# Another order for the projections, output rows and head buffers of a model's two mixing layers

## The chip, the cores and the metric

The kernel runs on one core of one Trainium2 chip. The metric is the device time of one execution in microseconds (us); lower is better.

## The reference

Two models of depth two run behind each other on 256 tokens of width 1024, in float32. The change concerns the second model's two mixing layers. Cut to what matters, one of them is:

```python
h = rms_norm(x, norm_mix_pre)
za, zq, zkv, zg, zc, zd = split(h @ w_in)
y_conv = silu(layer_norm(dwconv31(a * sigmoid(gate))))        # a, gate = halves of za
y_nsa = g0 * o_cmp + g1 * o_slc + g2 * o_win                  # 4 heads of 64, keys and values from zkv, g from zg
y_sgu = u * (w_s @ layer_norm(v) + b)                         # u, v = halves of gelu(zc)
y_pool = ((windowed means of zd) - zd) @ w_p * scale
x = x + rms_norm(concat(y_conv, y_nsa, y_sgu, y_pool) @ w_out)
```

`o_cmp` attends to 15 compressed blocks of keys; `o_slc` and `o_win` are causal attention over all 256 tokens here, with two different sets of keys and values. A feed-forward layer with its own norms follows each mixing layer.

## The kernel before

**Products.** A float32 weight is split into a high and a low part (`whi`, by ScalarE; `wlo`, by VectorE), activations likewise (`hh`/`hl`, `oh`/`ol`), and each product is three TensorE matmuls (`mm3`, line 821). Weights stream from memory through four buffers `wraw`; a chunk has one or two units of 128 x 1024, and at most six or seven converted units wait for use. `_plan` (line 138) lists the chunks in the order of use; `_weights` (line 68) takes those of the mixing layers from `MIX_ORDER` and `MIX_ROWS` (lines 57 and 58). One unit feeds 24 matmuls of 256 columns, a projection of 256 columns 48.

**Order of work.** Instructions are put on each engine's queue by a planner that runs on the host: a main line emits projections and output rows one after the other, and between their parts (`step`, line 787) it advances generators, which hold the elementwise chains, and converts further weights (`tick`, line 780). A generator goes on when its inputs are due by the planner's clock (`on`, line 766). The convolution's taps on VectorE come last: they fill what is left (`conv_gen`, line 1810).

**A mixing layer** (`mix`, line 2113). `begin` (line 999) computes the convolution's inputs ag0 and ag1 while the norm's statistics come in, and then makes the normalised input slice by slice, 8 slices of 128 channels, in `hh`/`hl` (`make_h`, line 939). Later projections read these. Then the main line follows `MIX_ORDER`:

- v and u: the gating's two halves. Their GELU is on ScalarE; `sgu_gen` (line 1901) does norm, spatial product and split, into slices 4 and 5 of `oh`/`ol`.
- conv: 18 of the 31 taps of one half of the convolution, as products with diagonal matrices. They wait for the gated input (`gated_input`, line 2147). The other taps are VectorE's; the norm, SiLU and split follow, into slices 0 and 1.
- cvf, kk, cw1, q, cvt: the heads' projections: inputs of the compression, keys (rotated, `rope2_gen`), the compression itself with raw weights (`nsa_cmp`, line 1951), queries, values and gates.
- zd: the pooled part's input; `pool_gen` (line 1870) does two small products, a scaling and the split, into slices 6 and 7.

**Heads** (`nsa_heads`, line 1980) run in two pairs, as generators that start once keys, queries, values and compression are there. A pair makes logits (TensorE), masks and maxima (VectorE), exponentials with sums (ScalarE), scaling by the gates (VectorE), transposes into `PT` (TensorE, copied by ScalarE), the products with the values, and the split into slices 2 and 3. Both pairs share the buffers `P` (probabilities) and `PT`; one mark, `busy`, is held from a pair's logits to its products with the values, so pair 2 begins behind pair 1's products.

**Rows.** The output projection takes four PSUM banks (`mm4`) and runs in four groups of 48 matmuls, one for each part: 0 is the convolution, 1 the heads, 2 the gating, 3 the pooled part. `MIX_ROWS` orders them; a group is emitted once its part is stored. The last group is followed at once by the norm behind the layer (`post`, line 1733).

Rows of the trace all carry one line number, 427, that of the call that records each operation; so work is followed by its tiles. `banks` is PSUM, `sv` and `su` the gating's v and u, `cs` the convolution's result before the split, `kp` the keys, `kr` and `qr` rotated keys and queries, `ps` the scaled pooled result (`banks<-pb,ar` is its last product), `cst,ar` a transpose of probabilities, `ar<-sg,gy` the gated input.

Of the kernel before, what the change touches and what calls it, by code (L numbers as in the profile page):

```python
# [53 lines left out]

FOX_ORDER = '0 1 f v0 2 3 v1 4 5 v2 6 7 v3'.split()

MIX_ORDER = 'v u conv cvf kk cw1 q cvt zd'.split()
MIX_ROWS = (2, 3, 0, 1)


DIL_TOKENS = ((3, 3, 3), (3, 3, 3), (3, 3, 3), (1, 1, 3))
# [6 lines left out]
def _weights(seg):  # L68
# [34 lines left out]
    elif kind == "mix":  # L103
        for which in ["ag0", "ag1"] + [w for w in MIX_ORDER if w != "conv"]:
            n = 1 if which in ("cvf", "kk") else 2
            out.append((("cw1", l) if which == "cw1" else ("mixt" if which in ("v", "cvt", "zd") else "mix", l, which), n))
        for c in MIX_ROWS:
            out.append((("row", ("w_out_2", (l,)), c * 256), 2))
# [561 lines left out]
class K:  # L670
# [1309 lines left out]
    def nsa_heads(self, t, q, qr, kr, vt, kc, vc, gates, pvs):  # L1980

        nc = self.nc
        half = [slice(0, 64), slice(64, 128)]

        where = {(0, 1): (0, 128), (1, 1): (128, 256), (0, 2): (384, 128), (1, 2): (512, 256),
                 (0, 0): (768, 16), (1, 0): (784, 16)}
        P, PT = self.PP, self.PT
        nm, sm, cf = self.small(12, "nm"), self.small(12, "sums"), self.small(12, "cf")
        cm = self.c("causal")

        while self.busy:
            yield
        self.busy.add(0)
        yield from self.on("pe", qr, kr, kc)
        for parts in (((0, 1), (1, 1)), ((0, 2), (1, 2), (0, 0), (1, 0))):
            L = yield from self.bank(2)
            o0 = where[parts[0]][0]
            for qt, br in parts:
                c0, n = where[qt, br]
                qs = slice(qt * 128, qt * 128 + 128)  # L2000
                for e, r in enumerate(half):
                    o = L[:, e, c0 - o0:c0 - o0 + n]
                    if br:
                        nc.tensor.matmul(o, qr[r, t, qs], kr[r, br - 1, :n], start=True, stop=True)
                    else:
                        nc.tensor.matmul(o[:, :15], q[r, t, qs], kc[r], start=True, stop=True)
            for e in range(2):
                n = 384 if len(parts) == 2 else 415
                yield from self.on("dve", L[:, e, :n], out=[P[e][:, o0:o0 + n]])
                for qt, br in parts:  # L2010
                    c0, n = where[qt, br]
                    i = e * 6 + qt * 3 + br
                    n = n if br else 15
                    if br:
                        mask = cm[:, 0:128] if qt == 0 else cm[:, 128:384]
                    else:
                        mask = self.c("cmask")[:, qt * 16:qt * 16 + 15]
                    nc.vector.tensor_tensor_reduce(P[e][:, c0:c0 + n], L[:, e, c0 - o0:c0 - o0 + n], mask, -1.0, CAP, OP.add,
                                                   OP.min, nm[:, i:i + 1])
            self.rel(L)  # L2020
        for e in range(2):
            yield from self.on("act", P[e])
            for (qt, br), (c0, n) in where.items():
                i = e * 6 + qt * 3 + br
                n = n if br else 15
                nc.scalar.activation(P[e][:, c0:c0 + n], P[e][:, c0:c0 + n], AF.Exp, scale=-1.0, bias=nm[:, i:i + 1],
                                     accum_out=sm[:, i:i + 1])
        yield from self.on("dve", sm)
        nc.vector.reciprocal(cf, sm)
        for e in range(2):  # L2030
            c3 = cf[:, 6 * e:6 * e + 6].rearrange("p (t b) -> p t b", t=2)
            h = 2 * t + e
            nc.vector.tensor_tensor(c3, c3, gates[:, :, h * 3:h * 3 + 3], op=OP.mult)
        for e in range(2):
            c = cf[:, 6 * e:6 * e + 6]
            for o, n, i in ((768, 15, 0), (0, 128, 1), (128, 256, 4)):
                if i == 0:
                    for qt in range(2):
                        p = P[e][:, 768 + 16 * qt:783 + 16 * qt]
                        nc.vector.tensor_scalar(p, p, c[:, 3 * qt:3 * qt + 1], None, op0=OP.mult)  # L2040
                    continue
                p = P[e][:, :768].rearrange("p (b n) -> p b n", b=2)[:, :, o:o + n]
                nc.vector.tensor_tensor(p, p, c[:, i:i + 2][:, :, None].to_broadcast([128, 2, n]), op=OP.mult)
        for e in range(2):
            pT = PT[:, e * 1024:e * 1024 + 1024]
            yield from self.on("pe", P[e])
            T = yield from self.bank()
            for i in range(4):
                nc.tensor.transpose(T[:, i * 128:i * 128 + 128], P[e][:, i * 128:i * 128 + 128], self.c("ident"))
            yield from self.on("act", T, out=[pT[:, 0:512]])  # L2050
            nc.scalar.copy(pT[:, 0:512], T)
            self.rel(T)
            T2 = yield from self.bank()
            for i in range(2):
                nc.tensor.transpose(T2[:, i * 128:i * 128 + 128], P[e][:, 512 + i * 128:640 + i * 128], self.c("ident"))
            for i in range(2):
                nc.tensor.transpose(T2[:15, 256 + i * 128:384 + i * 128], P[e][:, 768 + 16 * i:783 + 16 * i],
                                    self.c("ident"))
            yield from self.on("act", T2)
            nc.scalar.copy(pT[:, 512:768], T2[:, 0:256])  # L2060
            nc.scalar.copy(pT[:15, 768:1024], T2[:15, 256:512])
            self.rel(T2)
        yield from self.on("pe", PT)
        pv = yield from self.bank()
        x = PT.rearrange("p (e n) -> p e n", e=2)
        self.pv2(pv, [([vt[:, kt, br * 64:br * 64 + 64]] * 2, x[:, :, br * 384:br * 384 + 384], kt)
                      for br in range(2) for kt in range(2)], False)
        for e in range(2):
            nc.tensor.matmul(pv[64 * e:64 * e + 64, :S], vc, PT[:15, e * 1024 + 768:e * 1024 + 1024], start=False, stop=True,
                             skip_group_check=True)  # L2070
        self.busy.remove(0)
        pvs[t] = pv
        yield from self.o_store(pvs, 2 * t, 2 + t)
        if t:
            self.stored.add(1)
# [37 lines left out]
    def mix(self, l, norm, following):  # L2113
# [131 lines left out]
        def heads():  # L2245
            for t in range(2):
                self.pending.append((lambda: len(ready) == 3 and len(cmp) == 2,
                                     self.nsa_heads(t, v3(q), qr, kr, vt, kc, vc, gates, pvs)))
# [9 lines left out]
        heads()  # L2258
        for w in MIX_ORDER:
            f[w]()  # L2260
# [3 lines left out]
        def rows(i, c, after=None):  # L2264
            for half in range(2):
                self.wait(lambda: c in self.stored)
                w = self.st.get("row", ("w_out_2", (l,)), c * 256)
                x = (self.oh[:, 2 * c:2 * c + 2], self.ol[:, 2 * c:2 * c + 2])
                self.rows(acc, half, w, *x, i == 0, i == 3, after)
                if i < 3:  # L2270
                    self.tick()

        for i in range(3):
            rows(i, MIX_ROWS[i])
        return self.post(acc, lambda after: rows(3, MIX_ROWS[3], after), self.v("n_mix_post", l * 8, 8), following)

# [102 lines left out]
```

## Time and profile before

| | |
|---|---|
| median of 3 runs | 1850.83 us (1848.05 to 1851.8) |
| the profiled execution | 1849.76 us, span 1848.0 us |
| mean granted TensorE clock of the profiled execution | 0.996 |
| busy: TensorE matmul / weight load / VectorE / ScalarE | 98% / 95% / 80% / 54% |
| the chain that ended last | TensorE 67%, issue 18%, VectorE 10%, ScalarE 5% |
| first mixing layer: its first projection behind `begin` to its last rows | about 1231 to 1327 us |
| second mixing layer: the same | about 1544 to 1640 us |

PE is TensorE's matmul, PEld its weight load, DVE VectorE, ACT ScalarE, SP the queue that issues the weight loads. In a timeline a row shows start and length in us, engine, operation, output and inputs, shapes and count; the brackets at its end hold the idle time of that engine before it and what ended it. Ends of matmuls are modelled; their starts are measured.

### The profile page before, as it was taken

What the parts mean: (1) busy time and instruction counts of PE and PEld (TensorE: products, weight loads), DVE (VectorE), ACT (ScalarE), POOL (GpSimd) and SP (SyncE); (2) the same over time, 40 slices, a digit from 0 to 9 for tenths busy, and PEclk for the clock granted to TensorE, in tenths of its full rate; (3) what the DMA queues carried; (4) which work ended last, traced back from release to release, by engine and by line L of the source; (5) the groups of instructions that cost most, each with busy time, mean ns of one, the idle gap of its engine ahead of it and who ended that gap; (6) DMA issues with size and microseconds to landing.
All of it is one profiled execution on the core that took longest, in us unless ns stands there. A gap on an engine that the chain in (4) does not pass through costs nothing.

```text
span 1848.0 us, 36709 instructions
## 1 busy us (share of the span) xinstructions
PE 1801.9 (98%) x15239; PEld 1755.8 (95%) x15239; DVE 1479.2 (80%) x2696; ACT 1006.4 (54%) x1706; POOL 42.7 (2%) x51
## 2 busy tenths in 40 slices
PE   8999999999999999999999999999999999999997
PEld 7999999999999999999999999998899998889997
DVE  7978798898779867779788965589698779879876
ACT  4544568644454445555555654454676554566653
POOL 0200010000000000000000000000000000000000
PEclk9999999999999999999999999999999999999999
DMA  9889375499848973433333566533255543325550
GB/s 392 307 347 341 116 291 184 162 364 352 312 151 343 340 277 129 183 137 122 143 125 138 208 244 223 185 135 137 92 195 210 183 160 137 115 87 204 212 183 24
DMA packets 54474, 378.36 MB, mean 205 GB/s; under 512 B 6305, under 2 KB 7809, under 8 KB 9506
## 3 DMA queue, kind: packets, MB, share of 16 engines
q1 hardware_dynamic: 52992, 372.42, 54.5%
q0 software_dynamic: 1168, 3.46, 0.6%
q8 instruction: 119, 1.95, 0.4%
q14 instruction: 49, 0.40, 0.1%
q10 hardware_dynamic: 146, 0.14, 0.0%
HBM read 374.89 MB, written 1.05 MB: 203 GB/s over the span
## 4 chain that ended last, share of the span: by engine, by line
PE 67%; issue 18%; DVE 10%; ACT 5%; POOL 1%; DMA 0%; POOLq 0%; DVEq 0%; ACTq 0%
PE banks L427 67%; DVE ar L427 3%; DVE wlo L427 2%; ACT ar L427 1%; DVE x L427 1%; ACT whi L427 1%; POOL rz L427 1%; DVE sq L427 1%; DVE hl L427 1%; ACT L427 1%; ACT hh L427 1%; ACT sq L427 0%; DVE ht L427 0%; DVE rs L427 0%; DVE ol L427 0%
## 5 line engine op out<-in xcount | busy, mean ns | idle before, releaser
L427 DVE TENSOR_TENSOR wlo<-wraw,whi 128x1024 fp32r<-128x1024 f32 x557 | 669.8, 1220 | 173.8 <-ACT whi L427 172.8
L427 PE MATMUL banks<-hh,whi 128*128 128x256 f32 (+1 forms) x2792 | 792.2, 284 | 2.3 <-ACT whi L427 1.1
L427 PE MATMUL banks<-hh,wlo 128*128 128x256 f32 (+1 forms) x2792 | 782.4, 281 | 2.9 <-DVE wlo L427 2.9
L427 PE MATMUL banks<-hl,whi 128*128 128x256 f32 (+1 forms) x2792 | 782.2, 281 | 0.8 <-DVE hl L427 0.8
L427 ACT CAST whi<-wraw 128x1024 fp32r<-128x1024 f32 x557 | 569.4, 1048 | 181.6 <-DMA wraw<-w 93.4
L427 PEld LDWEIGHTS banks<-hh,whi 128*128 128x128 f32 x2792 | 525.6, 188 | 6.0 <-ACT hh L427 2.3
L427 PEld LDWEIGHTS banks<-hh,wlo 128*128 128x128 f32 x2792 | 526.0, 189 | 3.7 <-DVE wlo L427 3.7
L427 PEld LDWEIGHTS banks<-hl,whi 128*128 128x128 f32 x2792 | 526.4, 189 | 1.4 <-DVE hl L427 1.4
L427 PE MATMUL banks<-oh,whi 128*128 128x256 f32 x1312 | 372.7, 284 | 7.8 <-DVE x L427 3.5
L427 PE MATMUL banks<-ol,whi 128*128 128x256 f32 x1312 | 368.3, 281 | 4.0 <-DVE ol L427 3.8
L427 PE MATMUL banks<-oh,wlo 128*128 128x256 f32 x1312 | 367.7, 280 | 0.0
L427 PEld LDWEIGHTS banks<-oh,whi 128*128 128x128 f32 x1312 | 247.1, 188 | 15.6 <-DVE x L427 6.0
L427 PEld LDWEIGHTS banks<-ol,whi 128*128 128x128 f32 x1312 | 247.3, 188 | 4.9 <-DVE ol L427 4.9
L427 PEld LDWEIGHTS banks<-oh,wlo 128*128 128x128 f32 x1312 | 247.3, 188 | 0.0
L427 DVE CUSTOM_DVE_ANT_0 wraw<-wraw,cb 128x1024 f32<-128x1024 f32 x128 | 152.0, 1216 | 0.0
L427 ACT ACTIVATE sg<-banks 128x256 f32<-128x256 f32 x82 | 31.4, 384 | 163.9 <-PE banks L427 163.8
L427 PE MATMUL banks<-whi,hh 128*128 128x256 f32 x352 | 102.2, 290 | 1.6 <-ACT hh L427 1.4
L427 PE MATMUL banks<-whi,hl 128*128 128x256 f32 x352 | 99.1, 282 | 0.1
L427 PE MATMUL banks<-wlo,hh 128*128 128x256 f32 x352 | 98.8, 281 | 0.0
L427 DVE SCALAR_TENSOR_TENSOR cy<-cs,vec,cy 128x255 f32<-128x255 f32 (+1 forms) x176 | 83.7, 481 | 7.8 <-ACT cy L427 4.7
L427 DVE TENSOR_TENSOR sg<-banks,sg 128x256 f32<-128x256 f32 x82 | 34.4, 422 | 62.7 <-ACT sg L427 62.6
L427 ACT ACTIVATE cy<-cs,vec 128x256 f32<-128x256 f32 x88 | 47.9, 594 | 49.6 <-DVE cs L427 48.8
(214 smaller groups left out, 1734.1 us busy)
## 6 DMA issues: line engine op xcount, KB each, us to landing
wraw<-w SPq DMA_DIRECT2D x342, 1024.0 KB, 4.9
ar<-w SPq DMA_DIRECT2D x8, 1024.0 KB, 9.1
wraw<-w SPq DMA_DIRECT2D x5, 512.0 KB, 3.3
ar<-lw POOLq DMA_DIRECT2D x2, 752.0 KB, 5.1
x<-x SPq DMA_DIRECT2D x2, 512.0 KB, 4.8
out<-x SPq DMA_DIRECT2D x8, 128.0 KB, 1.9
ar<-bands POOLq DMA_DIRECT2D x1, 544.0 KB, 8.1
ar<-dm POOLq DMA_DIRECT2D x1, 512.0 KB, 9.1
```

The lines of the kernel that those rows point to most:

```text
L427: return f(out, *args, **kw)
```

## The change

Three things change. The projections are emitted as cvf, kk, conv, cw1, q, cvt, zd, v, u: the heads' first, then the pooled part, then the gating. The output rows come as pooled, gating, convolution, heads. And the heads hold two marks: 0 for the probabilities, from a pair's logits until its transposes are copied, and 1 for the transposed ones, from before the transposes to the products with the values. The weights' order in memory and on the load queue follows the first two.

```diff
-MIX_ORDER = 'v u conv cvf kk cw1 q cvt zd'.split()
-MIX_ROWS = (2, 3, 0, 1)
+MIX_ORDER = 'cvf kk conv cw1 q cvt zd v u'.split()
+MIX_ROWS = (3, 2, 0, 1)
@@ nsa_heads
-        while self.busy:
+        while 0 in self.busy:
             yield
         self.busy.add(0)
         yield from self.on("pe", qr, kr, kc)
...
                 nc.vector.tensor_tensor(p, p, c[:, i:i + 2][:, :, None].to_broadcast([128, 2, n]), op=OP.mult)
+        while 1 in self.busy:
+            yield
+        self.busy.add(1)
         for e in range(2):
             pT = PT[:, e * 1024:e * 1024 + 1024]
             yield from self.on("pe", P[e])
...
             self.rel(T2)
+        self.busy.remove(0)
         yield from self.on("pe", PT)
         pv = yield from self.bank()
...
-        self.busy.remove(0)
+        self.busy.remove(1)
         pvs[t] = pv
```

## Rows read from the trace of the kernel before

**Rows 1.** The page, busy us, share of the span and instructions by engine.

```profile
PE 1801.9 (98%) x15239; PEld 1755.8 (95%) x15239; DVE 1479.2 (80%) x2696; ACT 1006.4 (54%) x1706; POOL 42.7 (2%) x51
```

**Rows 2.** Busy by stretches: us; PE, PEld, DVE, ACT, POOL; clock; DMA share, GB/s.

```profile
1231.00:1283.10 52.10, 51.63 (x438) 48.40 (x437) 49.94 (x120) 26.75 (x55) 0.00 (x0) 1.00 0.49 182
...
1295.19:1303.36 8.17, 8.17 (x49) 6.83 (x49) 1.23 (x1) 5.29 (x10) 0.00 (x0) 0.63 0.36 129
...
1610.32:1615.67 5.35, 5.35 (x49) 4.31 (x49) 1.23 (x1) 3.99 (x8) 0.00 (x0) 1.00 0.57 199
```

**Rows 3.** Timeline of TensorE, first layer, around the pooled part's rows.

```profile
1291.10 1.03 PE L427 MATMUL banks<-pb,ar 128*128 128x256 f32 x4
1293.71 0.38 PE L427 MATMUL banks<-oh,whi 128*128 128x256 f32 x1 [1.58 <-ACT oh L427]
1295.19 0.58 PE L427 MATMUL banks<-ol,whi 128*128 128x256 f32 x1 [1.10 <-DVE ol L427]
```

**Rows 4.** Timeline of TensorE, second layer, pooled rows and pair 2's logits.

```profile
1610.32 0.39 PE L427 MATMUL banks<-ol,whi 128*128 128x256 f32 x1 [1.10 <-DVE ol L427]
...
1618.32 0.93 PE L427 MATMUL banks<-kr,qr 64*128 64x128 f32 x8 [0.89 <-DVE ol L427]
```

**Rows 5.** Timeline of TensorE, first layer, rotation of the keys and pair 2's transposes.

```profile
1257.67 0.70 PE L427 MATMUL banks<-kp,cst 128*128 128x256 f32 x2 [0.47 <-ACT kp L427]
...
1316.06 2.17 PE L427 MATMUL banks<-cst,ar 128*128 128x128 f32 x15 [0.26 <-DVE ar L427]
```

**Rows 6.** Timelines of TensorE and VectorE, start of the first and the second layer.

```profile
1230.93 0.28 PE L427 MATMUL banks<-whi,hh 128*128 128x256 f32 x1
...
1236.74 0.75 DVE L427 SCALAR_TENSOR_TENSOR ar<-sg,gy 128x256 f32<-128x256 f32 x2
...
1544.15 0.39 PE L427 MATMUL banks<-whi,hh 128*128 128x256 f32 x1 [1.41 <-ACT hh L427]
...
1549.10 0.42 DVE L427 TENSOR_TENSOR hl<-ht,hh 128x256 fp32r<-128x256 f32 x1 [0.19 <-ACT hh L427]
...
1550.86 0.28 PE L427 MATMUL banks<-whi,hl 128*128 128x256 f32 x1
1550.98 0.28 PE L427 MATMUL banks<-hh,whi 128*128 128x256 f32 x1
...
1552.91 0.75 DVE L427 SCALAR_TENSOR_TENSOR ar<-sg,gy 128x256 f32<-128x256 f32 x2
```

**Rows 7.** Timelines of ScalarE, TensorE and VectorE, first layer, the gating's chain.

```profile
1242.57 0.60 ACT L427 ACTIVATE su<-banks 128x512 f32<-128x512 f32 x1 [1.06 <-PE banks L427]
...
1243.70 1.14 PE L427 MATMUL banks<-ar,sv 128*64 128x128 f32 x16
...
1246.47 1.22 DVE L427 TENSOR_TENSOR wlo<-wraw,whi 128x1024 fp32r<-128x1024 f32 x1
1247.61 0.68 DVE L427 TENSOR_TENSOR ol<-sy,oh 128x512 fp32r<-128x512 f32 x1
```

**Rows 8.** Timeline of ScalarE, first layer: pair 1's exponentials, and the SiLU.

```profile
1277.76 1.28 ACT L427 ACT_TABLE_LOAD   x1 [1.74 <-DVE nm L427]
...
1283.65 0.19 ACT L427 ACTIVATION_READ_ACCUMULATOR ar<-ar,nm 128x1 f32 x1
...
1300.81 1.28 ACT L427 ACT_TABLE_LOAD   x1
1302.11 1.02 ACT L427 ACTIVATE cs<-banks,vec 128x256 f32<-128x256 f32 x2
```

**Rows 9.** First layer, convolution's end and its rows (timelines); heads' work (groups by tile).

```profile
1303.81 0.69 DVE L427 TENSOR_TENSOR ol<-cs,oh 128x512 fp32r<-128x512 f32 x1 [1.76 <-ACT oh L427]
...
1309.89 0.28 PE L427 MATMUL banks<-oh,whi 128*128 128x256 f32 x1
...
L427 DVE CUSTOM_DVE_ANT_0 ar<-banks,cst 128x128 f32<-128x128 f32 (+2 forms) x24 | 5.4, 290 | 0.0
L427 DVE TENSOR_TENSOR ar<-ar,cf 128x256 f32<-128x256 f32 (+1 forms) x8 | 4.1, 550 | 0.0
```

## The prediction

> **What bounds the kernel now.** I read the page first: TensorE is busy for 98% of the span [rows 1], so only the small rest, or a slower clock, can be won. The change touches the two mixing layers alone, so the busy table by stretches comes next. In the first layer's projections (1231.00 to 1283.10) TensorE is busy for 51.63 of 52.10 us and VectorE for 49.94 [rows 2]: two engines are full at once. The holes come after it, and the timeline of TensorE names them. The pooled rows wait 1.58 us for the high half of the pooled result and 1.10 us for its low half [rows 3]; the second layer repeats the pair, 1.58 (not shown) and 1.10 [rows 4]. The reader should see why: the pooled projection is the last one before the output rows, and only one group of rows (the gating's) stands between. Right behind these holes the clock falls in the first layer: the same 49 matmuls take 8.17 us at a mean granted clock of 0.63 (part of it at the lower level, 1.2 GHz), and 5.35 us at 1.00 (2.4 GHz) in the second [rows 2]. Smaller holes: 0.47 us ahead of the rotation of the keys, once in each layer; 0.26 us ahead of pair 2's transposes, once in each layer [rows 5]; 0.89 us for a PSUM bank, in the second layer alone [rows 4].
>
> **What the edit removes.** Matmul ends are modelled: in a stream a matmul is listed with 0.28 us while the next starts 0.12 us later [rows 6], so each listed hole is about 0.16 longer.
> - Pooled part. The new order has its projection before v and u, and its rows first. Two projections of 48 matmuls at 0.12, 11.4 us, then cover its chain; 3 us more than now would do. Gone: 1.58 + 1.10 + 2 x 0.16 = 3.0 us per layer, 6.0 in all. Should the cover fail, at most these 3.0 come back.
> - Clock. The holes ahead of the fall are gone, so I take back 8.17 - 5.35 = 2.8 us, once. Its bounds are 0 (another hole pulls it down) and 2.8.
> - Keys. Behind kk stood the compression's weights, with nothing between; now 18 convolution products do. Gone: 0.47 + 0.16 = 0.63 per layer, 1.3.
> - Pair 2. Heads start after cvt, and zd, v, u, 17 us of projections, lie behind them in place of zd alone. By the time the last rows want pair 2 it is long stored. Gone: 0.26 + 0.16 per layer, 0.8. The two marks let pair 2's logits start once pair 1's transposes are copied; in a queue with 17 us of cover this removes no TensorE wait by itself, 0 us (the copies would otherwise be covered too).
> - The bank: 0.89 + 0.16 = 1.05, bounds 0 and 1.05, since PSUM use around it changes; I take it, as two pairs no longer run beside the last rows.
>
> Sum removed: 6.0 + 2.8 + 1.3 + 0.8 + 1.05 = 12.0 us.
>
> **What the edit adds.** No arithmetic; each step is moved with all it issues. On SP's queue the weights go in the new order, cvf and kk as half chunks, and the compression's chunk holds one of four buffers for longer, until its products; behind kk follow the convolution's and the compression's products, which take no converted weights, so the stream gains a lead: 0. On POOL one memset of the blocks moves to an earlier place and has nothing queued behind it there: 0. On TensorE three things are late next.
> - The convolution's products need the gated input. In the first layer the projections start at 1230.93; cvf and kk take 48 x 0.12 = 5.7 and end at 1236.6; the input is written from 1236.74 for 0.75, to 1237.5 [rows 6]. Wait 0.9 us, which v and u (11.4 us) hid before.
> - In the second layer the normalised input is still being made when the projections start at 1544.15 [rows 6]. v takes each of its 8 slices for 6 matmuls (0.72 us), about the pace of making them, and u begins at 1550.98. cvf takes 3 per slice (0.36), so it outruns the maker and ends with it: the last low half is written from 1549.10 for 0.42 [rows 6], cvf ends near 1549.7, kk at 1552.5. The same 48 matmuls ended at 1551.1: 1.4 us lost. Then the gated input: 1552.91 + 0.75 = 1553.7, 1.1 us more. Together 2.5.
> - The gating's rows. u is now the last projection. From the GELU of u (1242.57) to the end of the gating's low half (1247.61 + 0.68) runs 5.7 us [rows 7]. The cover is one group of rows, 48 x 0.12 = 5.7, and the gating's own products, 1.14 [rows 7]: 6.9. But exponentials now run between v's and u's GELUs, so one more activation-table load may stand in the chain, 1.28 [rows 8], and a conversion of 1.2 [rows 7] may be ahead of it on VectorE, half of it on average. Wait: 5.7 + 1.3 + 0.6 - 6.9 = 0.7, rounded up to 1.0 for a queue that is full; 2.0 in all. Bounds: 0 (the load falls elsewhere) and 7.1 per layer (the rival below).
>
> A rule weighed: the load of 1.28 us at 1300.81 is followed by the next activation at 1302.11, 1.30 us in all [rows 8], and that is what I used. The Trainium skill, page "ScalarE: Activation LUTs", section "What ACT_TABLE_LOAD costs", puts a switch at about 2.66 us, load and drain, which speaks against an order with more switches; by it, an estimate, the wait would be 1.4 us longer per layer and the total 2.7 us higher. The row shows no such drain, so the row decides.
>
> Sum added: 0.9 + 2.5 + 2.0 = 5.4 us. Net: 12.0 - 5.4 = 6.6 us less. The profiled execution took 1849.76 us (span 1848.0), so 1843.2; the median of the three runs, 1850.83, is 1.1 above it, so 1844.3.
>
> **Rivals.**
> - Convolution late. Its taps take what VectorE has left, and VectorE is full. Now its low half is ready at 1303.81 + 0.69 = 1304.5 and its rows begin at 1309.89 [rows 9]: 5.4 us to spare. In the new order pair 2's work comes ahead of it, half of 5.4 for masks and half of 4.1 for scaling [rows 9], 4.8 us; and TensorE arrives 3.3 us earlier (half of 6.6). Were all of it in front, 4.8 + 3.3 - 5.4 = 2.7 us of new wait per layer: 1844.3 + 5.4 = 1849.7, no change. For it: 2.2 us idle in 52.1. Against it: the convolution's own chain after the taps sat behind the pooled holes too, and the gating's vector work moves behind it.
> - Slower: the gating behind pair 2. If u's GELU is queued on ScalarE behind pair 2's exponentials, their load and 12 exponentials run from 1277.76 to 1283.65 + 0.19, 6.1 us [rows 8]. It decides once pair 2's masks are done just before u ends. The wait before the gating's rows is then 7.1 us in place of 1.0, in both layers: 1844.3 + 12.2 = 1856.5; and 1862 if the clock falls behind both. At 3.2 us extra per layer the gain is gone. For it: pair 2 may start right around u. Against it: pair 1 starts 17 us of projections before u ends and pair 2 only behind pair 1's transposes, so its exponentials may as well be queued after u's GELU.
> - The order does less than it says: the clock falls anyway, say at the starved start of the second layer, and the bank wait stays: 2.8 + 1.05 back, 1848.2, still barely a gain.
>
> **The numbers.** A measurement of this kernel tells apart about 0.2%, 3.7 us, so faster means under 1847.1. Chances: my forecast 0.64 (1839 with nothing added, 1850.8 - 12.0, up to 1848 with the added waits two thirds larger); convolution late 0.18; the order does less 0.08; gating behind pair 2 0.10. Faster: nearly all of the first (0.62), a third of the second (0.06), half of the third (0.04): 0.72. Slower: 0.08 of the last and 0.02 of the second: 0.10. Same: 0.18. The range takes in the first three: 1839 to 1852; the likeliest case's own is 1839 to 1848.
>
> **What would show it.** In the profile after: no wait of TensorE on the pooled result in either layer; a clock of 1.00 through both layers; about 1 us of wait before the convolution's products; the second layer's first projection stretched to the pace of the normalised input; and, between the pooled and the gating's rows, a wait near 1 us. If that one is over 3 us, or the convolution's rows wait, the sum is wrong there; if the pooled wait stays, the first step is.

## The result and the profile after

The changed kernel takes 1865.8 us (median of 4 runs, 1864.99 to 1866.99) where the kernel before, run beside it, takes 1850.53: a ratio of 1.0083, 95% interval 1.0071 to 1.0096. It is slower by 0.8%; 1844.3 was forecast, with 1852 as the upper end. The profiled execution took 1866.99 us (span 1865.2).

The page's busy row, the answer to [rows 1]: the same matmuls, two more instructions on ScalarE, and TensorE's share one point lower.

```profile
PE 1809.7 (97%) x15239; PEld 1765.1 (95%) x15239; DVE 1479.8 (79%) x2696; ACT 1009.9 (54%) x1708; POOL 42.7 (2%) x51
```

Busy by stretches comes next, with one stretch for each mixing layer: from the norm's spread products (`banks<-cst,rz`) to the end of the last output rows. Columns as in [rows 2]. First the kernel before, then the changed one.

```profile
1224.69:1327.04 102.35, 98.72 (x807) 90.73 (x808) 82.16 (x215) 56.80 (x126) 0.79 (x1) 0.97 0.39 145
1542.02:1640.42 98.40, 91.75 (x759) 82.99 (x760) 80.78 (x214) 54.16 (x124) 0.79 (x1) 1.00 0.41 150
sum 200.75, PE 190.48 PEld 173.72 DVE 162.94 ACT 110.95 POOL 1.58; mean PE 95.24 PEld 86.86 DVE 81.47 ACT 55.48 POOL 0.79
```

```profile
1226.35:1333.63 107.28, 97.67 (x807) 90.48 (x808) 82.34 (x215) 59.44 (x128) 0.79 (x1) 0.95 0.38 138
1548.64:1657.63 108.99, 97.88 (x759) 89.30 (x760) 81.83 (x214) 58.13 (x127) 0.79 (x1) 0.91 0.36 126
sum 216.27, PE 195.56 PEld 179.77 DVE 164.18 ACT 117.58 POOL 1.58; mean PE 97.78 PEld 89.89 DVE 82.09 ACT 58.79 POOL 0.79
```

The first layer is 4.9 us longer, the second 10.6: 15.5 together, about the difference of the medians (15.3). The two profiled executions are 17.2 us apart; the other 1.7 lies ahead of the first layer, whose start moves between 1224.3 and 1228.9 us from one profiled execution to the next. In the second layer the clock, 1.00 before, is down to 0.91. This sum over the two layers is the measure that the experiments below are read with. It comes from one execution of each kernel: the kernel before and one of the experiments, alike in order, have 200.75 and 199.24, so a difference under some 2 us says little by itself.

TensorE's timeline has the holes. First layer, the rows with a wait over 0.3 us behind the layer's start, and the first pooled row:

```profile
1239.77 1.56 PE L427 MATMUL banks<-ar 128*128 128x256 f32 x6 [1.34 <-DVE ar L427]
...
1253.57 0.21 PE L427 MATMUL banks<-cst,cg 30*64 30x30 f32 x1 [0.73 <-ACT cg L427]
...
1275.81 0.87 PE L427 MATMUL banks<-cst,ar 128*128 128x128 f32 x4 [1.14 <-DVE ar L427]
...
1293.53 0.28 PE L427 MATMUL banks<-oh,whi 128*128 128x256 f32 x1
...
1304.24 0.30 PE L427 MATMUL banks<-cst,ar 128*128 128x128 f32 x1 [1.54 <-DVE ar L427]
...
1308.13 0.58 PE L427 MATMUL banks<-oh,whi 128*128 128x256 f32 x1 [2.33 <-ACT oh L427]
1310.94 0.58 PE L427 MATMUL banks<-ol,whi 128*128 128x256 f32 x1 [2.23 <-DVE ol L427]
```

The pooled rows (1293.53) start with no wait: the holes of [rows 3] are gone. In their place the gating's rows wait 2.33 us for the high and 2.23 us for the low half of the gating's result, and ahead of them pair 2's transposes, queued in front, wait 1.54. The second layer repeats it, with an idle 0.65 ahead of the transposes:

```profile
1628.03 0.30 PE L427 MATMUL banks<-cst,ar 128*128 128x128 f32 x1 [0.65 <-DVE ar L427]
...
1631.91 0.58 PE L427 MATMUL banks<-oh,whi 128*128 128x256 f32 x1 [2.32 <-ACT oh L427]
1634.72 0.58 PE L427 MATMUL banks<-ol,whi 128*128 128x256 f32 x1 [2.23 <-DVE ol L427]
```

Who is late shows on ScalarE's timeline, first layer. u's projection ends at 1293.69, and its GELU (`su`) starts at 1300.24:

```profile
1292.84 1.28 ACT L427 ACT_TABLE_LOAD   x1
1294.14 0.40 ACT L427 ACTIVATE ar<-ar,nm 128x128 f32<-128x128 f32 x1
...
1298.94 1.28 ACT L427 ACT_TABLE_LOAD   x1
1300.24 0.60 ACT L427 ACTIVATE su<-banks 128x512 f32<-128x512 f32 x1
...
1307.45 0.62 ACT L427 CAST oh<-sy 128x512 fp32r<-128x512 f32 x1 [0.95 <-DVE sy L427]
```

A load, pair 2's 12 exponentials and a second load, 7.4 us (1292.84 to 1300.22), stand ahead of it. On VectorE the rest of the gating's chain then finds pair 2's scaling and a conversion in front:

```profile
1301.80 1.23 DVE L427 TENSOR_TENSOR wlo<-wraw,whi 128x1024 fp32r<-128x1024 f32 x1 [5.05 <-ACT whi L427]
...
1304.89 1.02 DVE L427 TENSOR_TENSOR ar<-ar,cf 128x256 f32<-128x256 f32 x2
1305.82 0.87 DVE L427 SCALAR_TENSOR_TENSOR sy<-banks,vec,ar 128x256 f32<-128x256 f32 x2
...
1310.20 0.69 DVE L427 TENSOR_TENSOR ol<-sy,oh 128x512 fp32r<-128x512 f32 x1
```

When the gating's next vector step (`sy`) starts at 1305.82, the GELU has been done for 5 us (1300.84). What `sy` stands behind is the scaling and a conversion, and that conversion had waited 5.05 us for a cast that is queued on ScalarE behind the exponentials. From the GELU's start to the end of the low half it took 10.7 us; [rows 7] showed 5.7. Behind the holes the clock falls in both layers, where [rows 2] had it low in the first alone:

```profile
1305.50:1316.00 10.50, 5.95 (x27) 5.24 (x26) 5.46 (x9) 4.72 (x9) 0.00 (x0) 0.51 0.28 100
...
1630.00:1640.20 10.20, 6.06 (x26) 5.56 (x26) 5.17 (x8) 4.01 (x8) 0.00 (x0) 0.50 0.30 103
```

### The profile page after: what moved, and what is told of

It is laid out like the page before. It is cut to its first block, busy times and chain, and to the rows that moved or that the text cites. A ratio compares the mean times of both kernels' runs of the same rounds, so it can differ in the third digit from the quotient of the medians.

```text
span 1865.2 us, 36697 instructions
## 1 busy us (share of the span) xinstructions
PE 1809.7 (97%) x15239; PEld 1765.1 (95%) x15239; DVE 1479.8 (79%) x2696; ACT 1009.9 (54%) x1708; POOL 42.7 (2%) x51
## 4 chain that ended last, share of the span: by engine, by line
PE 66%; issue 18%; DVE 10%; ACT 4%; POOL 1%; DMA 0%; POOLq 0%; DVEq 0%; ACTq 0%
PE banks L427 66%; DVE ar L427 4%; DVE wlo L427 2%; DVE x L427 1%; DVE hl L427 1%; POOL rz L427 1%; ACT ar L427 1%; DVE sq L427 1%; ACT whi L427 1%; ACT L427 1%; ACT hh L427 1%; DVE ht L427 0%; ACT sq L427 0%; DVE sy L427 0%; DVE gy L427 0%
```

## The experiments

Two theories came out of this. **Q, the queues**: ScalarE and VectorE work in the order in which the planner emitted, so pair 2's softmax block (a load, 12 exponentials, scaling), emitted around the end of u, holds up whatever of the gating's chain stands behind it. **F, the front**: the heads' projections at the start of a layer outrun the vectors and the gated input that VectorE makes. Rivals: the two marks do it (M in the expectations); VectorE is over-full, as the heads' work now lies beside the convolution's taps (V); the order of the rows is too early for the gating in any case; the fallen clock does it (C).

All twelve experiments, behind the kernel before and the changed one, in one table. The order is that of `MIX_ORDER`, written where it differs from the changed kernel's; "layers" is the sum of both layers' stretches in the profiled execution (for pair 2 behind u that was the slowest of its ten, 1854.02 us); the medians of before beside them were 1849.75 to 1850.04 us.

| run | order of projections | rows | pair 2 | median, us | ratio, 95% interval | layers, us |
|---|---|---|---|---|---|---|
| before | v u conv cvf kk cw1 q cvt zd | 2301 | | 1850.53 | | 200.75 |
| changed | cvf kk conv cw1 q cvt zd v u | 3201 | | 1865.8 | 1.0083 [1.0071, 1.0096] | 216.27 |
| one mark | | 3201 | one mark | 1866.28 | 1.0084 [1.0068, 1.0101] | 215.9 |
| marks only | as before | 2301 | | 1850.42 | 1.0000 [0.9991, 1.0010] | 199.24 |
| rows 3021 | | 3021 | | 1849.13 | 0.9996 [0.9986, 1.0005] | 199.45 |
| pair 2 behind u | | 3201 | after u's projection | 1851.09 | 1.0008 [0.9999, 1.0017] | 203.7 |
| cvt first | cvt cvf kk conv cw1 q zd v u | 3201 | | 1865.54 | 1.0081 [1.0066, 1.0096] | 215.2 |
| cvt first, 3021 | same | 3021 | | 1850.37 | 1.0003 [0.9994, 1.0012] | 200.9 |
| filler | | 3201 | | 1865.02 | 1.0076 [1.0060, 1.0093] | 213.81 |
| zd last | cvt cvf kk conv cw1 q v u zd | 2031 | | 1869.86 | 1.0102 [1.0087, 1.0117] | 221.0 |
| gating first | cvt cvf kk conv cw1 q zd v u | 3201 | after the gating's store | 1847.83 | 0.9990 [0.9981, 0.9999] | 197.34 |
| q first | q cvf kk conv cw1 cvt zd v u | 3021 | | 1842.89 | 0.9968 [0.9956, 0.9981] | 193.88 |
| q first, gating first | same | 3201 | after the gating's store | 1848.82 | 0.9997 [0.9988, 1.0005] | 199.2 |
| cvt and q early | cvt cvf kk q conv cw1 zd v u | 3021 | | 1858.38 | 1.0052 [1.0039, 1.0066] | 207.6 |

### The marks

One mark: the new order and rows, with the heads' single mark of before.

```diff
-        while 0 in self.busy:
+        while self.busy:
             yield
...
-        while 1 in self.busy:
-            yield
-        self.busy.add(1)
...
-        self.busy.remove(0)
...
-        self.busy.remove(1)
+        self.busy.remove(0)
```

> The new order of projections and rows, with the one mark of the kernel before, so that pair 2 begins behind pair 1's products again. Theory Q (queue on ScalarE): the loss is u's GELU standing behind pair 2's twelve exponentials and two table loads; that order stays here, so 1862 to 1868 us, with the wait before the gating's rows at 4 us or more in each layer. Rival M (the marks let pair 2 in too early): 1850 us or less. Rival V (VectorE is over-full because the heads' work now lies beside the taps): 1860 us or more, as Q.

Marks only: the new marks, with the order and rows of before.

```diff
-MIX_ORDER = 'cvf kk conv cw1 q cvt zd v u'.split()
-MIX_ROWS = (3, 2, 0, 1)
+MIX_ORDER = 'v u conv cvf kk cw1 q cvt zd'.split()
+MIX_ROWS = (2, 3, 0, 1)
```

> The old order of projections and rows, with the two marks. Q and V: the marks by themselves move nothing that TensorE waits for but pair 2's start, 1848 to 1852 us. M: 1855 us or more.

With one mark the loss is the same, 1866.28 us, and the exponentials still stand ahead of u's GELU (load at 1295.61, GELU at 1302.99). The marks alone change nothing, 1850.42, and the pooled part's two holes are there again, 1.58 and 1.10 us. The order and the rows make the loss.

### Where the gating's rows stand, and what stands ahead of the gating

Rows 3021: the convolution's rows between the pooled and the gating's.

```diff
-MIX_ROWS = (3, 2, 0, 1)
+MIX_ROWS = (3, 0, 2, 1)
```

> The changed kernel with the output rows in the order pooled, convolution, gating, heads: the convolution's result is stored at 1295.6 us in the changed kernel's first layer, the gating's at 1310.9. Q: the convolution's 5.7 us of rows cover the gating's wait (2.33 + 2.23 us per layer) and with it most of the clock's fall behind it (about 10 us at half clock, some 5 us, per layer): 1846 to 1854 us. V: the wait moves to the convolution's rows or to pair 2's transposes, 1860 us or more.

Pair 2 behind u: the rows of the changed kernel, with pair 2 as a whole, from its logits on, let in only once u is projected.

```diff
-                self.pending.append((lambda: len(ready) == 3 and len(cmp) == 2,
+                self.pending.append((lambda t=t: len(ready) == 3 and len(cmp) == 2 and (t == 0 or u[0] is not None),
```

> The changed kernel, with pair 2 of the heads let in only once u's GELU is emitted, so that the GELU stands ahead of pair 2's exponentials on ScalarE and nothing else moves ahead of it. Q: the wait before the gating's rows falls under 1.5 us per layer, pair 2 is later but has two groups of rows as cover: 1846 to 1856 us. V: VectorE is as late as before, 1860 us or more, with the wait before the gating's rows still over 3 us.

Both remove nearly all of the loss. In the first the GELU is as late as ever (1298.42, behind a load at 1297.12), but 48 more matmuls cover it, and the gating's rows wait 1.41 us in all and 0.70 in the second layer; the layers go from 216.27 to 199.45, so the gating's early place, with the clock that falls behind it, costs 16.8 us, 8.0 and 8.8. The layers of rows 3021:

```profile
1224.52:1323.80 99.28, 94.66 (x807) 88.10 (x808) 81.89 (x215) 59.08 (x128) 0.79 (x1) 1.00 0.40 149
1538.82:1638.99 100.17, 93.69 (x759) 85.52 (x760) 81.48 (x214) 57.77 (x127) 0.79 (x1) 0.97 0.38 137
```

In the second nothing covers more, but the GELU and the gating's cast are ahead of pair 2's load, as ScalarE's timeline of that run shows:

```profile
1295.35 0.60 ACT L427 ACTIVATE su<-banks 128x512 f32<-128x512 f32 x1
1297.43 0.62 ACT L427 CAST oh<-sy 128x512 fp32r<-128x512 f32 x1 [1.48 <-DVE sy L427]
1299.01 1.28 ACT L427 ACT_TABLE_LOAD   x1
```

The gating's rows then don't wait, and pair 2's own do, the last ones, 2.15 us in the first layer and 0.96 in the second. An over-full VectorE (V) is not the cause: over both layers it is busy for 162.9 to 164.2 us in every run, slow or fast, and for 164.2 in the changed kernel and in this one alike.

### Which step of the chain has to be ahead

Cvt first takes one projection out from between q and v; with it come rows 3201 and, in a second kernel, 3021.

```diff
-MIX_ORDER = 'cvf kk conv cw1 q cvt zd v u'.split()
+MIX_ORDER = 'cvt cvf kk conv cw1 q zd v u'.split()
```

> The same projections, with the changed kernel's rows: pooled, gating, convolution, heads. Here u's GELU comes ahead of pair 2's exponentials by itself, since the heads start later. Q and F: although v and u are still the last projections and the gating's rows still second, the wait before these rows is under 2 us per layer: 1842 to 1850 us. If the place of v and u, right before their rows, were the cause, with whatever order on ScalarE: 1858 us or more.

> The rows pooled, convolution, gating, heads as in e3, and the projections cvt, cvf, kk, conv, cw1, q, zd, v, u: the values' projection, which takes 6 matmuls per slice, first. Theory F (front): in e3 the second layer needs 13.4 us from the norm's spread to the convolution's products for 48 projection matmuls, 4.3 more than the kernel before did for the same 48, and the first layer 1.5, because cvf and kk outrun the normalised input and the gated input; a projection at the pace of the slices ahead of them takes both away: 1841 to 1846 us, clock 1.00 at the second layer's start. Rival: the wait only moves to the heads, which start as late as before: 1848 us or more.

Both missed. In the one with rows 3201 the GELU does come ahead of the exponentials, and still the gating's rows wait 5.31 and 5.21 us. ScalarE, VectorE and TensorE of its first layer (timelines):

```profile
1296.47 0.60 ACT L427 ACTIVATE su<-banks 128x512 f32<-128x512 f32 x1
1297.08 1.28 ACT L427 ACT_TABLE_LOAD   x1
...
1303.06 0.60 ACT L427 CAST oh<-sy 128x512 fp32r<-128x512 f32 x1
...
1298.38 0.69 DVE L427 TENSOR_TENSOR sy<-sy,su 128x512 f32<-128x512 f32 x1
...
1308.67 0.69 DVE L427 TENSOR_TENSOR ol<-sy,oh 128x512 fp32r<-128x512 f32 x1
...
1309.41 0.58 PE L427 MATMUL banks<-ol,whi 128*128 128x256 f32 x1 [5.31 <-DVE ol L427]
```

The gating's product is done at 1299.07, but its cast is queued behind the load and the exponentials (1303.06), and its low half behind a conversion and pair 2's scaling (1308.67). So Q is wider than I had it: not the GELU alone, every step of the chain has to be ahead. With rows 3021 the start of the layers had no wait on the gated input, yet q, now last before the logits, makes them wait 1.62 us for its rotation in the first layer, in the second the gating's low half still comes 2.51 us late, and 1850.37 is no gain.

Gating first keeps cvt first and rows 3201 and takes pair 2, with all it issues, out of the chain's way.

```diff
-                self.pending.append((lambda: len(ready) == 3 and len(cmp) == 2,
+                self.pending.append((lambda t=t: len(ready) == 3 and len(cmp) == 2 and (t == 0 or 2 in self.stored),
```

> The run with cvt in front and rows 3, 2, 0, 1 (1865.5 us, 5.3 and 5.2 us of wait on the gating's last quarter), with one change: pair 2's softmax is issued only once the gating's whole chain is. Theory Q (any step of the gating's chain that stands behind pair 2's load, exponentials and scaling in the queues of ScalarE and VectorE is late): the wait ahead of and within the gating rows falls under 1.5 us in both layers, pair 2's own rows wait up to 2 us: 1846 to 1853 us. Rival (the rows' order is too early for the gating whatever stands ahead of it in the queues): the wait stays above 3 us, 1860 us or more.

1847.83 against 1865.54 us with one condition changed: 17.7 us, and 17.9 in the layers. Its layers, and ScalarE's and TensorE's timelines of the first:

```profile
1224.27:1323.73 99.46, 95.42 (x807) 88.81 (x808) 82.29 (x215) 57.91 (x127) 0.79 (x1) 1.00 0.42 149
1539.25:1637.13 97.88, 92.50 (x759) 85.49 (x760) 81.36 (x215) 55.50 (x125) 0.79 (x1) 0.97 0.43 151
```


```profile
1289.52 0.60 ACT L427 ACTIVATE su<-banks 128x512 f32<-128x512 f32 x1 [0.50 <-PE banks L427]
...
1293.95 0.62 ACT L427 CAST oh<-sy 128x512 fp32r<-128x512 f32 x1
1296.48 1.28 ACT L427 ACT_TABLE_LOAD   x1
...
1318.24 0.39 PE L427 MATMUL banks<-ol,whi 128*128 128x256 f32 x1 [2.15 <-DVE ol L427]
```

No gating row waits; pair 2's do (2.15 us), as Q says. The rows were not too early in any case: what stood ahead in the queues made them so. Not all of the 17.9 us is the gating's own wait: in cvt first the pooled rows waited 1.30 and 2.04 us until pair 2's maxima (`nm`) were done, and of that only 1.41 in the second layer, ended by `cz`, is left.

### The clock's share

Filler: 40 matmuls, whose results nobody reads, in front of the gating's first row, to keep TensorE at work in the hole.

```diff
+                if i == 1 and half == 0:
+                    self.busy_pe(40)
                 w = self.st.get("row", ("w_out_2", (l,)), c * 256)
```

> The changed kernel with 40 matmuls on constants (40 x 0.12 = 4.8 us) put on TensorE's queue right ahead of the gating's rows in both layers, where it now waits 2.33 + 2.23 us. If the clock falls because TensorE stands idle there (theory C), it stays at 1.00 behind them and the work behind takes some 2.5 us less per layer: 1859 to 1863 us. If not, the 4.8 us are filled and nothing comes back: 1865 us or more.

In the second layer the filler (5.06 us) took the hole's place and the clock stayed at 1.00, where the changed kernel had 0.50:

```profile
1630.00:1640.20 10.20, 9.05 (x75) 8.63 (x77) 6.03 (x12) 4.54 (x9) 0.00 (x0) 1.00 0.30 104
```

That layer came to 106.73 us, 2.3 under the changed kernel's. In the first the clock fell ahead of the filler, which then took 6.47 us, and the layer stayed at 107.08. The medians don't tell the two apart (1865.02 and 1865.8), and 1865 or more was the expectation's sign that nothing comes back. With the clock held behind the holes, 8.3 of the second layer's 10.6 us of loss remain. So the fallen clock is not the main cause (C), and its own price, 2.3 us in one layer of one execution, is hardly clear of the scatter.

### The front, and a faster order

Three more orders look for the rest. Zd last, with rows 2031:

```diff
-MIX_ORDER = 'cvf kk conv cw1 q cvt zd v u'.split()
-MIX_ROWS = (3, 2, 0, 1)
+MIX_ORDER = 'cvt cvf kk conv cw1 q v u zd'.split()
+MIX_ROWS = (2, 0, 3, 1)
```

> Projections cvt, cvf, kk, conv, cw1, q, v, u, zd and rows gating, convolution, pooled, heads: each part's rows stand at least 11 us of TensorE's work behind its projection or its vector work, both GELUs come together ahead of pair 2's exponentials. Q and F: no wait over 1.5 us on any part's rows, 1839 to 1845 us. V: the pair's transposes and the convolution wait for VectorE: 1848 us or more.

A miss, the slowest of all, and the time is the one that V expected: gating, pooled part, convolution and heads all meet at the end, and TensorE waits 4.15 (`cz`), 3.85, 3.74 (`oh`) and 5.59 us (`ol`) in the first layer. The second, with 2.72 and 2.07 as its longest waits, is 16 us shorter. VectorE does no more than elsewhere (163.7 us), so V is not it here either; which steps stood in each other's way no run takes apart. Cvt and q early:

```diff
-MIX_ORDER = 'cvf kk conv cw1 q cvt zd v u'.split()
-MIX_ROWS = (3, 2, 0, 1)
+MIX_ORDER = 'cvt cvf kk q conv cw1 zd v u'.split()
+MIX_ROWS = (3, 0, 2, 1)
```

> Order cvt, cvf, kk, q, conv, cw1, zd, v, u, rows 3, 0, 2, 1: both cvt and q in front of the convolution's products, u still last. Theory F: no wait in the front and none on the queries, 1843 to 1849 us. Rival: the convolution's products stand later and their activation falls behind pair 2's exponentials on ScalarE, so that the convolution's rows, put second, wait 2 us or more in each layer: 1851 to 1858 us.

Its rival's waits came, with a time just above its range (1858.38 us), by a longer way than its text has: the convolution's norm stands on VectorE behind a conversion whose cast is queued on ScalarE behind the exponentials, and its low half behind pair 2's scaling, the gating's product and one more conversion. VectorE and TensorE, first layer:

```profile
1293.48 1.22 DVE L427 TENSOR_TENSOR wlo<-wraw,whi 128x1024 fp32r<-128x1024 f32 x1 [3.28 <-ACT whi L427]
...
1301.56 0.38 PE L427 MATMUL banks<-oh,whi 128*128 128x256 f32 x1 [1.76 <-ACT oh L427]
...
1304.77 0.39 PE L427 MATMUL banks<-ol,whi 128*128 128x256 f32 x1 [2.83 <-DVE ol L427]
```

The convolution's rows, second in line, wait 4.6 us: the same block, another victim. Q first moves only q, to the front, with rows 3021:

```diff
-MIX_ORDER = 'cvf kk conv cw1 q cvt zd v u'.split()
-MIX_ROWS = (3, 2, 0, 1)
+MIX_ORDER = 'q cvf kk conv cw1 cvt zd v u'.split()
+MIX_ROWS = (3, 0, 2, 1)
```

> Order q, cvf, kk, conv, cw1, cvt, zd, v, u, rows 3, 0, 2, 1. Theory F (the rest of the loss of the run with these rows lies in the start of a layer, where cvf and kk, fed by the vectors normalised a few hundred ns before, have nothing of their own behind them): the 8 slices of q take 1.7 us that the hidden vectors' eviction and the gated input need, so the wait on the gated input goes from 1.34 and 2.15 us to under 0.5 in both layers and no wait on the queries takes its place, since q stands at the front: 1842 to 1847 us. Rival: q's rotation on VectorE stands ahead of the keys' and of the gated input there and delays both; a wait of 1 us or more comes up before the convolution's products or the logits: 1848 to 1852 us.

1842.89 us, faster than both kernels, as F expected. Busy by stretches, its two layers:

```profile
1225.77:1322.78 97.01, 94.37 (x807) 87.87 (x808) 82.05 (x215) 58.98 (x128) 0.79 (x1) 1.00 0.41 153
1538.39:1635.26 96.87, 93.09 (x759) 85.23 (x760) 81.05 (x214) 56.82 (x126) 0.79 (x1) 0.96 0.41 153
```

They are 5.6 us shorter than with rows 3021 alone, and no wait on the gated input is left. The GELU is still behind the exponentials here (1297.40, behind a load at 1296.10); the two groups of rows ahead leave 0.82 us of wait on the gating's low half, and 0.45 in the second layer. What the front is bound by shows in VectorE's timeline of the rows 3021 run, second layer, where the convolution's products start at 1552.22 after 2.15 us of wait:

```profile
1546.25 1.28 DVE L427 TENSOR_TENSOR gy<-banks,rb 128x512 f32<-128x512 f32 x2
1547.44 1.22 DVE L427 TENSOR_TENSOR wlo<-wraw,whi 128x1024 fp32r<-128x1024 f32 x1
1548.58 1.66 DVE L427 TENSOR_TENSOR ar<-banks,ar 64x240 f32<-64x240 f32 x4
1550.27 0.43 DVE L427 SCALAR_TENSOR_TENSOR ar<-sg,gy 128x256 f32<-128x256 f32 x1
1550.61 1.22 DVE L427 TENSOR_TENSOR wlo<-wraw,whi 128x1024 fp32r<-128x1024 f32 x1
1551.75 0.42 DVE L427 SCALAR_TENSOR_TENSOR ar<-sg,gy 128x256 f32<-128x256 f32 x1
```

Ahead of the gated input stand cvf's four evictions (1.66 us), and between its halves a conversion. cvf and kk end earlier in this run than in the changed kernel (the last matmul of kk starts 8.84 us behind the first of cvf, there 9.83, at a lower clock), and the products still start 13.4 us behind the norm's spread in both. So this low clock cost nothing: VectorE's queue sets that start.

Last, both remedies at once:

```diff
-MIX_ORDER = 'cvf kk conv cw1 q cvt zd v u'.split()
+MIX_ORDER = 'q cvf kk conv cw1 cvt zd v u'.split()
...
-                self.pending.append((lambda: len(ready) == 3 and len(cmp) == 2,
+                self.pending.append((lambda t=t: len(ready) == 3 and len(cmp) == 2 and (t == 0 or 2 in self.stored),
```

> Order q, cvf, kk, conv, cw1, cvt, zd, v, u with the changed kernel's own rows 3, 2, 0, 1, and pair 2's softmax issued once the gating's whole chain is: both remedies, for the front and for the queue. By Q and F together 1842 to 1849 us. By Q alone (the front not mended by q) 1848 to 1852. If neither holds, 1858 us or more.

1848.82 us lies in both ranges that the expectation gives, so it does not decide between them, and it is no better than rows 3021 alone: holding pair 2 back makes its own rows, the last ones, wait 2.15 us in both layers. With q first the cover of rows 3021 is 5.9 us cheaper than the hold (1842.89).

## Why the prediction was wrong

Along the runs the loss splits like this, in the layers: q first gives 200.75 - 193.88 = 6.9 us, the front without q ahead costs 5.6 of it (199.45 - 193.88), and the gating's early place 16.8 more (216.27 - 199.45): -6.9 + 5.6 + 16.8 = 15.5, the loss seen. The sum closes by construction, so it is a split and no proof; the medians give 6.9, 6.2 and 16.7. That 6.9 is near the 6.6 forecast as the net is chance: that net was 12.0 off and 5.4 on, for another order.

- **The pooled wait: right.** Gone in both layers, and back when the old order is (marks only).
- **Keys' rotation: right.** No wait there. **The bank: half right.** The wait before pair 2's logits is gone, but it is gone in marks only too, so it need not be the order that removed it, and in q first 1.01 and 1.04 us stand there (ended by `cz`). And ahead of the second layer's pooled rows stands one of 0.70 us that pair 2's maxima (`nm`) end, probably for a bank again.
- **The marks at 0: right,** and shown alone.
- **Pair 2's transposes: wrong.** 0.26 us in [rows 5] became 1.54 and 0.30 in the first layer, 0.65 and 0.30 in the second. I had pair 2 "long stored" by then; it was in the middle of its scaling.
- **The gating's rows at 1.0 us per layer: the step that failed.** I let one more table load into the chain and half a conversion; there were two loads, 12 exponentials, pair 2's scaling and three conversions of weights on VectorE. In the sum the GELU starts when u ends and the chain takes 5.7 + 1.3 + 0.6 = 7.6 us from there, against a cover of 6.9; measured, the GELU starts 6.5 us after u's end (1293.69 to 1300.24) and the chain takes 10.7 more. The rows' own waits are 2.33 + 2.23 + 2 x 0.16 = 4.9 us per layer, and with the transposes ahead and the clock behind it is 8.0 and 8.8. This is the slower rival, which I gave 0.10: it "decides once pair 2's masks are done just before u ends", and pair 2's load started at 1292.84, 0.9 us before u's projection ended. I argued against it that the exponentials "may as well be queued after u's GELU"; the planner fixes the order of emission on the host before the run, so it could have been worked out, and that was the weak point. The rival had the GELU alone behind the block; cvt first, with the GELU ahead of it, loses as much, so the cast and the vector steps behind the block count as well. Its price of 7.1 was near (with the transposes ahead the holes come to 7.0 and 6.1 us), its total short: 1856.5 to 1862 against 1865.8, as the fronts came out 2.4 us larger and pair 1's transposes waited too (both below).
- **The clock, 2.8 us taken back: wrong.** It fell in the first layer once more (0.51 over 10.5 us) and in the second anew. The bound "another hole pulls it down" held. The 2.8 itself was the price of one execution: with the same order and the same two holes, marks only lost 1.2 us less behind them (last section).
- **The fronts, 0.9 and 2.5 us: mis-sized.** 1.34 + 0.16 = 1.5 in the first. In the second the products start 13.4 us behind the norm's spread, and before the same 48 matmuls had ended after 9.1 [rows 6]: 4.3 lost. I took the gated input's time over from before; cvf's evictions (1.66 us), moved ahead of it with cvf, were not counted.
- **Not foreseen:** 0.73 us for the compression's GELU in the first layer, 1.14 and 1.94 for pair 1's transposes. Part of them stays in q first (0.81 and 0.42 on the transposes).
- **The convolution late: no.** Its low half was ready at 1295.6, and no row of it waited in the changed kernel. It comes true where its products are moved back (cvt and q early).
- **The rule on table loads.** The new loads are followed by the next activation after 1.30 us again (1292.84 to 1294.14, 1298.94 to 1300.24), and start within 0.02 us of the end of the instruction ahead. The Trainium skill, page "ScalarE: Activation LUTs", section "What ACT_TABLE_LOAD costs", has about 2.66 us for a switch; no load here showed it, so the row rightly decided, and the loss has another cause: the number of instructions ahead.

Open: how the 5.6 us of the front divide between gated input, compression and pair 1's transposes, and whether a version with pair 2 held only in part beats q first, weren't tried.

## What to carry to other kernels

When a chain is moved to the end, list what each in-order queue holds between its steps at that point: a block of another chain that was harmless earlier (a softmax: a table load, 12 exponentials, scaling) delays any step that lands behind it, and there are two remedies, to give the chain one more group of cover or to hold the block back. Which is cheaper has to be tried: cover was by 2.0 us with the changed kernel's projections (1849.13 against 1851.09, held until u) and by 5.9 with q first, the hold by 2.5 with cvt first (1847.83 against 1850.37). When a projection moves to the front, its evictions move too; look at what the vector engine owed others there. A small net gain worked out from many terms deserves a check of the one term whose upper bound exceeds it.

## What the runs showed of the hardware that was not expected

The granted clock falls behind some holes and not behind others like them: with the same idle time at the second layer's start (1.41 and 1.42 us, no second hole over 0.2), it stayed at 1.00 in the kernel before (1544.15 to 1550.98) and was 0.79 over the first projection in gating first. Nor is the price of a fall the same each time: behind the first layer's two holes (1.58 and 1.10 us in both) the same work, from the row with the 1.10 to the next `kr,qr`, takes 8.10 us in the kernel before (1295.19 to 1303.29) and 6.89 in marks only (1294.95 to 1301.84); in the second layer before, at 1.00, it takes 5.28. And a low clock is not always a price: at 0.66 and 0.83 over cvf and kk (changed kernel, rows 3021) the next product started equally late, since it waited for VectorE. The two windows, of gating first and, behind it, of the changed kernel:

```profile
1541.38:1549.37 7.99, 7.94 (x50) 7.41 (x51) 7.80 (x19) 5.15 (x10) 0.00 (x0) 0.79 0.50 208
```

```profile
1550.77:1560.88 10.11, 9.71 (x48) 8.49 (x48) 9.85 (x23) 5.44 (x11) 0.00 (x0) 0.66 0.14 58
```
